# Attention's finished head pairs split one at a time, and one eviction of v moved behind a transpose

## The chip, the core and the metric

The kernel runs on one core of one Trainium2 chip. The metric is the device time of one execution in microseconds; the median of the runs shown is compared. The core has five engines that are used here: TensorE (PE in the profile; its weight loads are listed apart as PEld), VectorE (DVE), ScalarE (ACT), GpSimd (POOL) and SyncE (SP), which issues most DMAs. Each engine runs its own instructions in a fixed order and waits on semaphores for the others.

## The reference

A trunk of two layers over 512 tokens of width 1024: the first mixes with attention that has a forgetting gate, the second with a short gated convolution. A squared-ReLU MLP and a gated embedding follow in each. The change lies in the first layer's attention alone:

```python
def fox_attention(h, w_in, b_f, w_out):
    proj = h @ w_in                       # q, k, v and the forget logits
    ...
    log_f = jax.nn.log_sigmoid(f_logit)
    c = lax.cumsum(log_f, axis=1).transpose(0, 2, 1)
    ...
        s = jnp.einsum('bhqd,bhkd->bhqk', qb, k, preferred_element_type=jnp.float32)
        s = s + cb[..., :, None] - c[..., None, :]
        s = jnp.where(k_pos[None, :] <= q_pos[:, None], s, NEG_INF)
        pr = jax.nn.softmax(s, axis=-1)
        return jnp.einsum('bhqk,bhkd->bhqd', pr.astype(v.dtype), v)
    ...
    return o @ w_out
```

There are 16 heads of 64 columns, and the 512 queries are taken in four blocks of 128.

## The kernel before

All products are made exact by splitting: a 32-bit operand becomes a high half (hi), which ACT makes with a copy into the float32r type, and a low half (lo), the rest, which DVE makes with a subtraction. `mm3` (L266) then runs three matmuls, hi·hi, lo·hi and hi·lo. So each operand of a product costs one ACT and one DVE instruction, and each tile that leaves PSUM the same.

SBUF holds a pool of 70 pages of 128x512, from which nearly all tiles come; PSUM has 8 banks. Where an engine's order is not written out by hand (`tc.manual_schedule`), a scheduler orders the instructions when the kernel is built: earlier code has priority, an instruction whose inputs aren't expected yet lets later ones pass, and pages are handed out in the order of the code. `add_manual_dep(..., NoSync, ...)` (L634) fixes an order between two instructions of one engine without a semaphore.

*The start* (L700 to L732, order by hand on PE, DVE, ACT and POOL). The normalized input of four token blocks is turned by TensorE transposes (`turn_rows`, L696; `turned`, L334) and kept in two large tiles hT.hi and hT.lo (hTh and hTl in the profile; `keep`, L340). In between run the products for the first 272 columns of v (`values`, L461): block t of v is made in six groups of four matmuls (L479), and the transposes of block t + 1 stand before one of the groups (L476). Each block's result is evicted by `keep_v` (L485): a logit on DVE (L487), two casts on ACT (L500) and two subtractions on DVE (L502), none of which issues a DMA. `values` gives `keep_v` back, and the list `done_v` holds it until its turn. `prepare(n)` (L175) loads weights up to number n and splits them (L285 on ACT, L287 on DVE).

*The main loop* (L757 to L773). A step c takes one head and one of four key blocks (c // 4 and c % 4). `turn` (L576) transposes the softmax weights into a PSUM bank (pT, L579) and splits them into ph and pl (L583, that is L276 and L277). `mix` (L587), two steps later, multiplies them with v (L598, L599); after the fourth block the head's output leaves PSUM (L603, L604) and with every second head a pair is finished and enters the list `complete`. `scores` (L556) runs eight steps ahead (L563 to L572), `bias` (L538) further still. Between these, `next(main)` runs a piece of the generator `stream` (L656): first the q and k projections of the head pairs 1 to 7 (`project`, L510, eight products for k and eight for q, each followed by a `yield`; it evicts to kh, kl and qs), two pieces in each step, then the output product (`out_part`, L641) for token block 0, block 1, and at last pair 6.

The output product needs the finished pairs as a split operand. They are written over hT, whose row k holds the input of projection product k, so a pair's split must wait until the last projection has read that row. `split_o` (L614) does this only from the start of `out_part` (`streaming`): the casts of all finished pairs at once (L622), five of them at that point. `low_o` (L625) makes their subtractions (L629) when the first product needs one, and for the later pairs behind the `turn` of every fourth step (L767).

For the last eight steps (L758) TensorE's order is by hand too.

Of the kernel before, what the change touches and what calls it, by code (L numbers as in the profile page):

```python
# [8 lines left out]
F32 = mybir.dt.float32  # L9
F32R = mybir.dt.float32r  # L10
AF = mybir.ActivationFunctionType
ALU = mybir.AluOpType
# [3 lines left out]
P = 128  # L16
D = 1024
S = 512
# [3 lines left out]
KT = D // P  # L22
# [46 lines left out]
def trunk(ctx: ExitStack, tc, x, pT, g, gT, wv, wqk, bf, wo, wci, wcq, cw, wco, wup, wdn, wpp, wpg, out):  # L69
    nc = tc.nc  # L70
# [9 lines left out]
    def page(name, dtype=F32):  # L80
        return pages.tile([P, S], dtype, tag="pg", name=name)
# [78 lines left out]
    def derive(key):  # L160
        at, sums = recipes.pop(key)
        fetch(max(at.values()) + 1)
        B = {name: fetched[n][:, :S] for name, n in at.items()}
        for name, a, b, op in sums:
            t = page("_".join(str(u) for u in (*key, *name)))
            derived[(*key, *name)] = t
            B[name] = t[:, :S]
            ins = nc.gpsimd.tensor_tensor(out=B[name], in0=B[a], in1=B[b], op=op)  # L168
            if last_norm:
                tc.add_manual_dep(  # L170
                    ins.ins, last_norm.pop().ins.name,
                    mybir.DependencyInfo(mybir.DependencyClass.Sync, mybir.DependencyReason.DATA),
                )

    def prepare(upto, lows=None):  # L175
        while begun[0] < min(upto, len(order)):
            n = begun[0]
            begun[0] += 1
            key, at = order[n]
            for of in (key[:3], key[:2]):  # L180
                if of in recipes:
                    derive(of)
            hi, lo = page(f"wh{n}", F32R), page(f"wl{n}", F32R)
            if isinstance(at, tuple):
                raw, w = derived.pop(key), S
                eng = nc.gpsimd if (key[0] == "dn" and key[2] > 0) or key[-1] in ON_POOL else nc.vector
            else:
                fetch(at + 1)
                raw, eng, w = fetched[at], lows or nc.vector, loads[at].shape[-1]
                fetched[at] = None  # L190
            if key[0] in ("v", "qk"):
                split_gained(hi, lo, raw, w, key[2], eng, key[0] == "qk" or key[1] == 2)
            else:
                split(hi[:, :w], lo[:, :w], raw[:, :w], eng)
            ready[key] = Pair(hi[:, :w], lo[:, :w])
# [78 lines left out]
    def split(hi, lo, src, eng=nc.vector):  # L274

        nc.scalar.copy(hi, src)  # L276
        return eng.tensor_tensor(out=lo, in0=src, in1=hi.bitcast(F32), op=ALU.subtract)  # L277
# [135 lines left out]
    def attention(hT, first_x, b_f, work, by_hand):  # L413
# [94 lines left out]
        stacked, probs, outs, both = {}, {}, {}, {}  # L508

        def project(i):  # L510

            heads = [[page(f"{n}{i}_{e}", F32R) for n in ("qs", "kh", "kl")] for e in range(2)]
            stacked[i] = heads
            for s in (1, 0):
                ps = bank(f"qk{i}_{s}")
                for k in range(KT):
                    mm3(
                        ps, narrow("qk", i, k=k, c=s * P),
                        hT.at(lambda h: h[:, k, :]), k == 0, k == KT - 1,
                    )  # L520
                    if k < KT - 1:
                        yield
                for e in range(2):
                    a, b = slice(64 * e, 64 * e + 64), slice(64 - 64 * e, 128 - 64 * e)
                    q, kh, kl = heads[e]
                    if s == 0:
                        nc.scalar.mul(q[a, :S], ps[a, :], HD**-0.5)
                        nc.vector.scalar_tensor_tensor(
                            out=q[b, :S], in0=ps[a, :], scalar=HD**-0.5,
                            in1=q[a, :S].bitcast(F32), op0=ALU.mult, op1=ALU.subtract,  # L530
                        )
                    else:
                        split(kh[a, :S], kl[a, :S], ps[a, :])
                        for h in (kh, kl):
                            nc.sync.dma_start(h[b, :S].bitcast(F32), h[a, :S].bitcast(F32))
                yield
# [39 lines left out]
        def turn(h, j):  # L576
            ps = bank(f"pT{h}_{j}")
            for b in range(j, NB):
                nc.tensor.transpose(  # L579
                    ps[:, b * P : (b + 1) * P], probs[h][b][:, j * P : (j + 1) * P], ident  # L580
                )
            ph, pl = page(f"ph{h}_{j}", F32R), page(f"pl{h}_{j}", F32R)
            ins = split(ph[:, j * P : S], pl[:, j * P : S], ps[:, j * P :])  # L583
            weights[h, j] = (ph, pl)
            return ins

        def mix(h, j):  # L587

# [21 lines left out]

        banks_o = {}
        oT, complete, lows, streaming = [], [], [], [True]

        def split_o():  # L614

            if streaming:
                return
            if not oT:
                oT.append(turned_x)
            while complete:  # L620
                k = complete.pop(0)
                nc.scalar.copy(oT[0].hi[:, k, :], outs[k][:, :S])  # L622
                lows.append(k)

        def low_o(behind=None):  # L625

            while lows:
                k = lows.pop(0)
                ins = nc.vector.tensor_tensor(  # L629
                    out=oT[0].lo[:, k, :], in0=outs.pop(k)[:, :S],  # L630
                    in1=oT[0].hi[:, k, :].bitcast(F32), op=ALU.subtract,
                )
                if behind is not None:
                    tc.add_manual_dep(  # L634
                        ins.ins, behind.ins.name,
                        mybir.DependencyInfo(
                            mybir.DependencyClass.NoSync, mybir.DependencyReason.DATA
                        ),
                    )

        def out_part(ts, ks):  # L641

            streaming.clear()
            split_o()
            for k in ks:
                if k in lows:
                    low_o()
                for t in ts:
                    for n in range(2):
                        if (t, n) not in banks_o:  # L650
                            banks_o[t, n] = bank(f"o{n}_{t}")
                        w = wide("o", n, k, soon=O_SOON)
                        mm3(banks_o[t, n], tokens(oT[0], k, t), w, k == 0, False)
                        yield

        def stream():  # L656
            for i in range(1, KT):
                yield from project(i)
            yield from out_part((0,), range(6))
            yield from out_part((1,), range(6))  # L660
            prepare(where["o", 1, KT - 1] + 1)
            yield from out_part((0, 1), (6,))

        name = "n0"
        E, done_v = mybir.EngineType, []
# [30 lines left out]
        def turn_rows(t, hs):  # L696
            for n in range(2):
                keep(t, n, turned(t, n, hs[n], name), hT)

        with tc.manual_schedule(engines={E.PE, E.DVE, E.Activation, E.Pool}):  # L700
            work(12)
            r = inverse(0, mean_squares(0))
            prepare(2)
            hs = scale_rows(0, r)
            prepare(4)
            ps0 = [turned(0, n, hs[n], name) for n in range(2)]
            nc.scalar.copy(hT.hi[:, :4, :P], quads(ps0[0]))
            v = mean_squares(1)
            keep_low(0, ps0[0])
            prepare(5)  # L710
            r = inverse(1, v)
            nc.scalar.copy(hT.hi[:, 4:, :P], quads(ps0[1]))
            hs1 = scale_rows(1, r)
            prepare(KT)
            keep_low(1, ps0[1])
            v = mean_squares(2)
            r = inverse(2, v)
            done_v.append(values(0, 0, lambda: turn_rows(1, hs1)))
            hs2 = scale_rows(2, r)
            v = mean_squares(3)  # L720
            r = inverse(3, v)
            done_v.append(values(0, 1, lambda: turn_rows(2, hs2)))
            hs3 = scale_rows(3, r)
            prepare(KT + 2)
            done_v.pop(0)()
            done_v.append(values(0, 2, lambda: turn_rows(3, hs3)))
            prepare(KT + 4)
            done_v.pop(0)()
            prepare(KT + 6)
            done_v.append(values(0, 3, lambda: None))  # L730
            done_v.pop(0)()
            prepare(KT + 8)  # L732
# [5 lines left out]
            out=ones[:, :S], in_=ones[:, :S], compare_op=ALU.is_ge, fill=0.0, base=0,  # L738
# [403 lines left out]
    oT = lhs  # L1142
# [121 lines left out]
```

## Time and profile before

| | us |
|---|---|
| median of 3 runs | 1223.75 (1223.65 to 1224.49) |
| the profiled execution | 1223.06 |
| its span, first to last instruction | 1221.2 |
| mean granted TensorE clock | 0.998 |

In timelines a line has the start, the duration, the engine, the line of the kernel, the operation and its operands, output before input, then the number of instructions merged into the line and in brackets the idle time before it with what ended it. Matmuls have their columns in the shape (128x512). A row "x8" begins with the first of eight. A matmul's end is modelled, so the distance between starts tells more than the duration.

The start of v's products lies at 7 to 23 us, the main loop with the heads at about 80 to 225 us, the output product between 193 and 257 us.

### The profile page before, as it was taken

What the parts mean: (1) busy time and instruction counts of PE and PEld (TensorE: products, weight loads), DVE (VectorE), ACT (ScalarE), POOL (GpSimd) and SP (SyncE); (2) the same over time, 40 slices, a digit from 0 to 9 for tenths busy, and PEclk for the clock granted to TensorE, in tenths of its full rate; (3) what the DMA queues carried; (4) which work ended last, traced back from release to release, by engine and by line L of the source; (5) the groups of instructions that cost most, each with busy time, mean ns of one, the idle gap of its engine ahead of it and who ended that gap; (6) DMA issues with size and microseconds to landing.
All of it is one profiled execution on the core that took longest, in us unless ns stands there. A gap on an engine that the chain in (4) does not pass through costs nothing.

```text
span 1221.2 us, 18759 instructions
## 1 busy us (share of the span) xinstructions
PE 1209.6 (99%) x6202; PEld 1030.4 (84%) x6202; DVE 922.9 (76%) x1466; ACT 682.4 (56%) x1457; POOL 653.9 (54%) x612
## 2 busy tenths in 40 slices
PE   8999999999999999999999999999999999999997
PEld 7888887898888888888889999989888888888886
DVE  7668888586779766879877789766876787669873
ACT  5567778558634563455566434545756345635551
POOL 1036666154887777775213355216677878778210
PEclk9999999999999999999999999999999999999999
DMA  8556554623244224428123023552421443235401
GB/s 279 153 159 165 166 142 125 203 93 104 79 138 132 85 71 128 138 78 293 60 92 124 29 88 104 158 171 70 138 79 63 135 139 97 66 113 181 164 11 59
DMA packets 86161, 148.73 MB, mean 122 GB/s; under 512 B 10224, under 2 KB 17952, under 8 KB 86064
## 3 DMA queue, kind: packets, MB, share of 16 engines
q1 hardware_dynamic: 85488, 147.01, 39.2%
q8 instruction: 49, 0.80, 0.3%
q10 hardware_dynamic: 576, 0.53, 0.1%
q14 instruction: 48, 0.39, 0.1%
HBM read 136.93 MB, written 6.37 MB: 117 GB/s over the span
## 4 chain that ended last, share of the span: by engine, by line
PE 91%; issue 2%; DVE 2%; ACT 2%; POOL 1%; DMA 1%; POOLq 0%; DVEq 0%; ACTq 0%
PE up L269 9%; PE up L268 9%; PE up L270 9%; PE dn L268 8%; PE dn L269 8%; PE dn L270 8%; PE qk L269 2%; PE qk L270 2%; PE qk L268 2%; PE pg L268 2%; PE pg L269 2%; PE pg L270 2%; PE pT L579 1%; PE co L270 1%; PE co L269 1%
## 5 line engine op out<-in xcount | busy, mean ns | idle before, releaser
L277 DVE TENSOR_TENSOR wl<-raw,wh 128x512 fp32r<-128x512 f32 x346 | 347.4, 1049 | 14.2 <-ACT wh L276 13.5
L269 PE MATMUL up<-hTh,wl 128*128 128x512 f32 (+1 forms) x576 | 210.2, 365 | 0.0
L270 PE MATMUL up<-hTl,wh 128*128 128x512 f32 (+1 forms) x576 | 209.6, 365 | 0.0
L268 PE MATMUL up<-hTh,wh 128*128 128x512 f32 (+1 forms) x576 | 208.7, 366 | 0.0
L276 ACT CAST wh<-raw 128x512 fp32r<-128x512 f32 x346 | 189.4, 625 | 4.5 <-DVE xd L373 4.4
L924 ACT ACTIVATE r<-up 128x512 f32<-128x512 f32 (+1 forms) x72 | 39.4, 547 | 205.0 <-PE up L270 205.0
L277 POOL TENSOR_TENSOR wl<-dn_T,wh 128x512 fp32r<-128x512 f32 x96 | 132.5, 1412 | 30.0 <-ACT wh L276 30.0
L268 PEld LDWEIGHTS up<-hTh,wh 128*128 128x128 f32 x576 | 108.6, 189 | 17.7
L269 PEld LDWEIGHTS up<-hTh,wl 128*128 128x128 f32 x576 | 108.6, 189 | 17.5
L168 POOL TENSOR_TENSOR dn_T<-raw,raw 128x512 f32<-128x512 f32 x56 | 86.1, 1548 | 69.1 <-DMA raw<-in_wdn 56.7
L270 PEld LDWEIGHTS up<-hTl,wh 128*128 128x128 f32 x576 | 108.3, 189 | 17.4
L970 DVE TENSOR_TENSOR acc<-dn,acc 128x512 f32<-128x512 f32 x168 | 107.4, 679 | 16.0 <-PE dn L270 16.0
L168 POOL TENSOR_TENSOR dn_T<-raw,dn_T 128x512 f32<-128x512 f32 x56 | 91.9, 1640 | 2.2
L276 ACT CAST wh<-dn_T 128x512 fp32r<-128x512 f32 x112 | 61.4, 616 | 11.0 <-POOL dn_T L168 11.0
L277 DVE TENSOR_TENSOR A12l<-q,A12h 128x512 fp32r<-128x512 f32 x28 | 22.0, 787 | 54.4 <-ACT A12h L276 54.4
L984 POOL TENSOR_TENSOR acc<-acc,acc 128x512 f32<-128x512 f32 x28 | 46.9, 1706 | 9.9 <-DVE acc L970 9.9
L270 PE MATMUL qk<-hTl,wh 128*128 128x512 f32 x128 | 50.8, 397 | 0.0
L269 PE MATMUL qk<-hTh,wl 128*128 128x512 f32 x128 | 50.8, 397 | 0.0
L268 PE MATMUL qk<-hTh,wh 128*128 128x512 f32 x128 | 50.7, 396 | 0.0
L269 PE MATMUL pg<-wh,hTl 128*128 128x512 f32 x128 | 50.5, 394 | 0.0
L268 PE MATMUL pg<-wh,hTh 128*128 128x512 f32 x128 | 50.4, 394 | 0.0
L277 DVE TENSOR_TENSOR A11l<-q,A11h 128x256 fp32r<-128x256 f32 x28 | 22.9, 820 | 36.1 <-ACT A11h L276 36.1
(404 smaller groups left out, 3303.2 us busy)
## 6 DMA issues: line engine op xcount, KB each, us to landing
raw<-in_wup SPq DMA_DIRECT2D x128, 256.0 KB, 3.0
raw<-in_wdn SPq DMA_DIRECT2D x128, 256.0 KB, 2.9
raw<-in_wcq SPq DMA_DIRECT2D x36, 256.0 KB, 2.8
raw<-in_wqk SPq DMA_DIRECT2D x32, 256.0 KB, 4.0
raw<-in_wpg SPq DMA_DIRECT2D x32, 256.0 KB, 3.8
g<-in_g SPq DMA_DIRECT2D x22, 256.0 KB, 5.2
prl<-neg_c SPq DMA_DIRECT2D x16, 256.0 KB, 6.5
raw<-in_wo SPq DMA_DIRECT2D x16, 256.0 KB, 5.3
```

The lines of the kernel that those rows point to most:

```text
L168: ins = nc.gpsimd.tensor_tensor(out=B[name], in0=B[a], in1=B[b], op=op)
L268: nc.tensor.matmul(ps, a.hi, b.hi, start=start, stop=False)
L269: nc.tensor.matmul(ps, a.lo, b.hi, start=False, stop=False)
L270: nc.tensor.matmul(ps, a.hi, b.lo, start=False, stop=stop)
L276: nc.scalar.copy(hi, src)
L277: return eng.tensor_tensor(out=lo, in0=src, in1=hi.bitcast(F32), op=ALU.subtract)
L579: nc.tensor.transpose(ps[:, b * P : (b + 1) * P], probs[h][b][:, j * P : (j + 1) * P], ident)
L924: nc.scalar.activation(r[:, :n], ps[:, :n], AF.Relu)
L970: ins = nc.vector.tensor_tensor(out=a, in0=banks[s], in1=a, op=ALU.add)
L984: nc.gpsimd.tensor_tensor(out=a, in0=a, in1=acc[i, s][:, :S], op=ALU.add)
```

## The change

`turn` no longer calls the helper `split`; it issues the same two instructions itself and keeps the newest of each in `latest`. `split_o` takes a finished pair only up to number `reach[0]`; for the pairs 0 to 5 it queues the cast behind the newest ph cast on ACT and issues the subtraction at once, queued behind the newest pl subtraction on DVE. `reach` is set from within the last projection: after its q product of row 1 pair 0 may go, after row 3 pair 1, after row 5 pair 2, after row 7 pair 3; in `out_part` it is k + 3. Since two pieces run in each step, pairs 0 to 4 come up in steps 44 to 48, behind the turns of steps 43 to 47; pair 5 comes up in step 50. Pairs 6 and 7 are split as before. Separately, `keep_v` of block 0 is issued after block 2's products and the transposes of block 3 instead of before them.

```diff
@@ -580,9 +580,13 @@
             ph, pl = page(f"ph{h}_{j}", F32R), page(f"pl{h}_{j}", F32R)
-            ins = split(ph[:, j * P : S], pl[:, j * P : S], ps[:, j * P :])
+            latest[0] = nc.scalar.copy(ph[:, j * P : S], ps[:, j * P :])
+            latest[1] = nc.vector.tensor_tensor(
+                out=pl[:, j * P : S], in0=ps[:, j * P :], in1=ph[:, j * P : S].bitcast(F32),
+                op=ALU.subtract,
+            )
             weights[h, j] = (ph, pl)
-            return ins
+            return latest[1]
@@ -610,6 +614,7 @@
         oT, complete, lows, streaming = [], [], [], [True]
+        reach, latest = [0], [None, None]
@@ -617,12 +622,21 @@
-            while complete:
+            while complete and complete[0] <= reach[0]:
                 k = complete.pop(0)
-                nc.scalar.copy(oT[0].hi[:, k, :], outs[k][:, :S])
+                ins = nc.scalar.copy(oT[0].hi[:, k, :], outs[k][:, :S])
                 lows.append(k)
-
-        def low_o(behind=None):
+                if k < 6:
+                    behind(ins, latest[0])
+                    low_o(latest[1])
+
+        def behind(ins, other):
+            tc.add_manual_dep(
+                ins.ins, other.ins.name,
+                mybir.DependencyInfo(mybir.DependencyClass.NoSync, mybir.DependencyReason.DATA),
+            )
+
+        def low_o(after=None):
@@ -630,19 +644,16 @@
-                if behind is not None:
-                    tc.add_manual_dep(
-                        ins.ins, behind.ins.name,
-                        mybir.DependencyInfo(
-                            mybir.DependencyClass.NoSync, mybir.DependencyReason.DATA
-                        ),
-                    )
+                if after is not None:
+                    behind(ins, after)
 
         def out_part(ts, ks):
 
             streaming.clear()
             split_o()
             for k in ks:
+                reach[0] = k + 3
+                split_o()
                 if k in lows:
                     low_o()
@@ -655,7 +666,12 @@
         def stream():
             for i in range(1, KT):
-                yield from project(i)
+                for n, _ in enumerate(project(i)):
+                    yield
+                    if i == KT - 1 and n > KT:
+                        streaming.clear()
+                        reach[0] = (n - KT - 1) // 2
+                        split_o()
             yield from out_part((0,), range(6))
@@ -722,8 +738,8 @@
             prepare(KT + 2)
+            done_v.append(values(0, 2, lambda: turn_rows(3, hs3)))
             done_v.pop(0)()
-            done_v.append(values(0, 2, lambda: turn_rows(3, hs3)))
             prepare(KT + 4)
```

## The prediction

> **What bounds the kernel now.** I read the page first: engine busy times, then the chain of waits.
>
> ```profile
> PE 1209.6 (99%) x6202; PEld 1030.4 (84%) x6202; DVE 922.9 (76%) x1466; ACT 682.4 (56%) x1457; POOL 653.9 (54%) x612
> PE 91%; issue 2%; DVE 2%; ACT 2%; POOL 1%; DMA 1%; POOLq 0%; DVEq 0%; ACTq 0%
> ```
>
> TensorE is the bound, and the change leaves its instructions as they are. So only time in which TensorE stands still can be won. Busy time hides most of that, because a matmul's shown duration covers the gap behind it; I therefore read starts. Two neighbouring 512-column products start 0.23 us apart (193.48 and 193.71 below), so 256 columns are worth 0.11 and 128 columns 0.06. Then I went to the timelines at the two places that the diff touches.
>
> At the end of attention (PE, then ACT, then DVE):
>
> ```profile
> 182.03 0.27 PE L579 MATMUL pT<-ident,prl 128*128 128x128 f32 x1
> ...
> 189.88 0.27 PE L564 MATMUL sc<-kl,qs 128*128 128x128 f32 x1
> 190.22 0.39 PE L598 MATMUL ps_o<-ph,v 128*128 128x256 f32 x1
> 190.82 0.33 PE L579 MATMUL pT<-ident,pr 128*128 128x128 f32 x1 [0.21 <-DVE nmx L566]
> ...
> 191.55 0.39 PE L563 MATMUL sc<-kh,qs 128*128 128x256 f32 x1 [0.18 <-DVE kl L277]
> 191.77 0.28 PE L564 MATMUL sc<-kl,qs 128*128 128x256 f32 x1
> 192.00 0.39 PE L599 MATMUL ps_o<-pl,v 128*128 128x256 f32 x1
> ...
> 193.48 0.39 PE L268 MATMUL o<-wh,hTh 128*128 128x512 f32 x1
> 193.71 0.40 PE L269 MATMUL o<-wh,hTl 128*128 128x512 f32 x1
> ...
> 199.23 0.40 PE L270 MATMUL o<-wl,hTh 128*128 128x512 f32 x1
> ```
>
> ```profile
> 183.63 0.62 ACT L622 CAST hTh<-oT 128x512 fp32r<-128x512 f32 x1 [0.56 <-PE qk L269]
> ...
> 185.91 1.13 ACT L622 CAST hTh<-oT 128x512 fp32r<-128x512 f32 x2
> ...
> 187.42 1.14 ACT L622 CAST hTh<-oT 128x512 fp32r<-128x512 f32 x2
> ...
> 189.80 1.03 ACT L276 CAST ph<-pT 128x256 fp32r<-128x256 f32 x3
> ...
> 197.15 0.37 ACT L276 CAST ph<-pT 128x256 fp32r<-128x256 f32 x1
> ```
>
> ```profile
> 184.28 0.69 DVE L629 TENSOR_TENSOR hTl<-oT,hTh 128x512 fp32r<-128x512 f32 x1 [0.45 <-PE qk L269]
> ...
> 187.01 1.29 DVE L629 TENSOR_TENSOR hTl<-oT,hTh 128x512 fp32r<-128x512 f32 x2
> 188.22 0.68 DVE L277 TENSOR_TENSOR kl<-qk,kh 64x512 fp32r<-64x512 f32 x1
> 188.82 1.28 DVE L629 TENSOR_TENSOR hTl<-oT,hTh 128x512 fp32r<-128x512 f32 x2
> ...
> 190.80 0.69 DVE L277 TENSOR_TENSOR kl<-qk,kh 64x512 fp32r<-64x512 f32 x1
> ...
> 193.57 0.16 DVE L571 RECIPROCAL rs<-sm 128x1 f32<-128x1 f32 x1 [0.56 <-ACT prr L570]
> ...
> 197.16 0.69 DVE L528 SCALAR_TENSOR_TENSOR qs<-qk,qs 64x512 fp32r<-64x512 f32 x1 [0.45 <-ACT qs L527]
> ...
> 199.54 0.29 DVE L277 TENSOR_TENSOR pl<-pT,ph 128x128 fp32r<-128x128 f32 x1 [1.24 <-ACT ph L276]
> ```
>
> What to see: the five splits (five casts on L622, five subtractions on L629) stand between 183.6 and 190.1. The transposes of one turn ended at 182.3 (182.03 + 0.27), yet their cast ph runs only at 189.80, behind all five casts, and then three turns come at once. On DVE four of the five subtractions stand ahead of the two kl subtractions of the last projection. From 189.88 to 192.00 TensorE does 0.06 + 0.11 + 3 × 0.11 + 2 × 0.11 = 0.7 us of work in 2.1 us: 1.4 us are lost.
>
> **Part one: v's eviction behind the last transposes.**
>
> ```profile
> 16.08 1.03 PE L337 MATMUL n_p<-ident,n_h 128*128 128x128 f32 x8
> ...
> 19.48 0.67 PE L479 MATMUL v<-wl,hTh 128*128 128x272 f32 x4
> 19.99 1.03 PE L337 MATMUL n_p<-ident,n_h 128*128 128x128 f32 x8
> 20.78 0.74 PE L479 MATMUL v<-wh,hTl 128*128 128x272 f32 x4
> 21.83 0.77 PE L479 MATMUL v<-wh,hTh 128*128 128x272 f32 x4 [0.30 <-ACT hTh L276]
> ```
>
> ```profile
> 16.72 1.08 ACT L276 CAST hTh<-n_p 128x512 fp32r<-128x512 f32 x2 [3.32 <-PE n_p L337]
> ...
> 20.85 0.43 ACT L500 CAST v<-v 128x128 fp32r<-128x128 f32 x2 [1.83 <-DVE logit L487]
> 21.17 1.10 ACT L276 CAST hTh<-n_p 128x512 fp32r<-128x512 f32 x2
> ```
>
> ```profile
> 19.33 1.41 DVE L287 SCALAR_TENSOR_TENSOR wl<-raw,first_g,wh 128x512 fp32r<-128x512 f32 x2
> ...
> 21.81 1.29 DVE L277 TENSOR_TENSOR hTl<-n_p,hTh 128x512 fp32r<-128x512 f32 x2
> ```
>
> Four 272-column products take 0.51 us (19.48 to 19.99), so TensorE is free at 20.78 + 0.51 = 21.29 and stands until 21.83: 0.54 us. It waits for hTh, whose cast stands on ACT behind v's two casts, which stand behind the logit on DVE. The block before shows the free case: transposes at 16.08, cast at 16.72, 0.64 us later. So the cast can start at 19.99 + 0.64 = 20.63 instead of 21.17, and hTh is there at about 21.29, when TensorE is free. Removed: 0.54 us.
>
> The price: the moved step (one logit, two casts, two subtractions, no DMA) now stands behind hTl, 1.29 us on DVE, and the next weight casts on ACT stand behind it, as do the loads that wait for their raw buffers: some 0.8 us later. What covers them is six groups of 0.51 us of the last v block and the two weights whose low halves end at 20.74 (19.33 + 1.41), each good for 3 × 0.23 = 0.7 us per block of tokens. That is 4.5 us from 21.29 with one block alone. Cover gone, the lateness of 0.8 would eat the gain: bounds −0.54 and +0.3. I take **−0.5**, since the cover is five times the delay.
>
> **Part two: the splits one by one.** Nothing is added or removed: five casts at 0.57 us (1.13 / 2) and five subtractions at 0.65 us (1.29 / 2). They move behind the turns of steps 43 to 47, released as the last projection passes their rows of hT.
>
> The stall at 190: the kl subtractions then have no split ahead of them (four × 0.65 = 2.6 us of DVE and four × 0.57 = 2.3 us of ACT gone from 185.9 to 190.1), so ph comes earlier by up to 2.6 us. I value the stall of 1.4 at −1.2, leaving 0.2 for the handovers that every turn has; bounds −1.4 and 0 (if the projection's products, which filled TensorE meanwhile, are merely spread otherwise).
>
> Later there is more:
>
> ```profile
> 205.89 0.28 PE L564 MATMUL sc<-kl,qs 128*128 128x256 f32 x1
> 206.46 0.33 PE L579 MATMUL pT<-ident,prr 128*128 128x128 f32 x1 [0.29 <-DVE pl L277]
> ...
> 210.92 0.40 PE L269 MATMUL o<-wh,hTl 128*128 128x512 f32 x1
> 211.67 0.51 PE L270 MATMUL o<-wl,hTh 128*128 128x512 f32 x1 [0.35 <-DVE wl L277]
> ```
>
> Here TensorE loses 0.46 (0.57 − 0.11) and 0.52 (0.75 − 0.23) because DVE is late, while DVE had stood idle for 1.24 us at 199.54. The reason is the run of output products from 193.48 to 199.23, four pairs' worth. After the change a fourth pair may enter only behind the turn whose ph runs at 197.15. Its six products, 6 × 0.23 = 1.4 us, then stand behind that turn instead of ahead; attention and with it DVE restart up to 1.4 us sooner, and these products are left over for the thin steps after 199.5. Bounds: −1.4 and, if DVE must first do the postponed subtractions, +3.2 (five × 0.65). DVE's idle rows above (0.56 + 0.45 + 1.24 = 2.2 us) take in most of those, so I value it near the lower end, **−1.1**.
>
> The new waits: each cast is queued behind the newest ph on ACT, each subtraction behind the newest pl on DVE. Behind them stand the exponentials of later scores and the next ph. The sixth pair's subtraction moves ahead by some turns, inside a stretch where DVE is full anyway: nothing, or ±0.65, one subtraction.
>
> A rule that speaks against this part: the row at 183.63 shows ACT standing 0.56 us before the first split, for a projection product that still reads that row of hT. The Trainium skill, "TensorE: Matmul & The Clock Gate", section "Architectural detail: the array is 16× 32×32, not 1× 128×128", says that ACT and DVE serve their queues strictly in order, TensorE alone pulling weight loads ahead. By that rule a split that waits so holds ph and the exponentials too; its result is the third rival. This row agrees: ACT did nothing meanwhile.
>
> **Sum.** The profiled execution took 1223.06 us, 1.86 around its span of 1221.2; the median is 0.69 above it. 1223.06 − 0.5 − 1.2 − 1.1 = 1220.3, and 1220.3 + 0.69 = **1221.0 us** against 1223.75. Nothing downstream absorbs it: TensorE is the chain from there on.
>
> **Rivals.**
> 1. *The splits aren't the cause at 199 and later.* DVE is simply full there, and the lows move from one full stretch into the next. For it: 2.2 us of idle against 3.2 us of lows. Then only 0.5 + 1.2 come: 1222.0.
> 2. *The change doesn't do what it says.* The splits stand between other work already (one, two, two), and TensorE's order stays the same: only v's part counts, 1223.2. Against it: ph at 189.80 follows the last of them.
> 3. *The splits wait at the head of ACT.* Each of the five waits 0.56 us as the first did: +2.8, with v's −0.5 and no other gain 1226.05. Against it: four of the five showed no such wait.
> 4. *The output products lose their pairs (slower).* Place: the run from 193.48. With three pairs released instead of four it is 1.4 us too short for the wait that it covers, and five lows of 0.65 stand ahead of pl instead of in gaps: 1.4 + 3.25 = 4.65; less 0.5 and 1.2 it is +2.95, 1226.7. It decides as soon as DVE's 2.2 us of idle are not where the lows arrive. For it: the lows are tied to pl, the very chain that starts the next turn. Against: shorter delay at 190 leaves projection products over, each 0.7 us, for the same gap.
> 5. *All stalls go* (the lows fit in gaps, the later stalls vanish whole, 1.4 more than the sum): 1219.6.
>
> **How the numbers follow.** About 0.2%, 2.45 us, is what a measurement of this kernel can tell from no change: below 1221.3 is faster, above 1226.2 slower. My forecast gets 0.50 (its own range 1220.0 to 1222.0; 0.35 of it below 1221.3), rival five 0.05, rival one 0.11, rival two 0.06, rival three 0.06 (half of it above 1226.2), rival four 0.22. Faster: 0.35 + 0.05 = 0.40. Slower: 0.22 + 0.03 = 0.25. The same: 0.35. The range 1219.5 to 1226.3 leaves out a little of rival five and most of rival four, some 0.2; it is wide because of the bounds +3.2 and −1.4 on the postponed lows.
>
> **What would show it.** Right: the first v product of the last block starts near 21.3 and ACT's hTh cast ahead of v's casts; the first split behind a ph, none between the kh casts; no gap over 0.3 us between 187 and 192 by the old clock; the run of output products cut to three pairs and no DVE idle over 1 us around 199. Wrong: a gap of over 1 us in front of an output product that waits for hTl, an idle ACT in front of L622 several times, or DVE busy without a break from 190 to 215 while TensorE loses as much as before. If the time is above 1223.2, part two's sign was wrong.

## The result and the profile after

| | before | after |
|---|---|---|
| median, us (12 runs each) | 1223.81 (1223.65 to 1224.63) | 1221.28 (1220.75 to 1222.23) |
| profiled execution, us | 1223.06 | 1220.75 |
| its span, us | 1221.2 | 1219.0 |

The ratio is 0.9979, with a 95% interval from 0.9971 to 0.9988: 2.53 us less by the medians, 2.31 by the profiled executions. The page's busy times and chain hardly differ, which is how a change reads that only takes gaps out of the bounding engine:

```profile
PE 1208.5 (99%) x6202; PEld 1030.3 (85%) x6202; DVE 919.2 (75%) x1466; ACT 684.0 (56%) x1457; POOL 653.8 (54%) x612
PE 92%; issue 2%; DVE 2%; ACT 2%; POOL 1%; DMA 0%; POOLq 0%; DVEq 0%; ACTq 0%
```

TensorE runs the same products, so the start of the same product in two traces tells how far one kernel is ahead of the other. This table is used for all that follows: start in before minus start in the kernel named, in us.

| product | before, start | after | v alone | splits alone | unqueued | casts free | at once | two by two |
|---|---|---|---|---|---|---|---|---|
| first projection product | 59.55 | 0.64 | -0.18 | 0.02 | 0.19 | 0.45 | 0.37 | -0.14 |
| transposes of the last turn | 221.17 | 2.15 | -0.59 | 1.54 | -0.33 | 0.15 | -4.16 | -0.69 |
| between the two | | +1.51 | -0.41 | +1.52 | -0.52 | -0.30 | -4.53 | -0.55 |

Two executions of one text (the O_SOON 3 of below) gave +0.76 and +0.59 between the two products, so a difference of 0.2 is not read as an effect here, and a run that comes out at -0.3 or -0.5 is read as one that won none of the 1.5. Whole times of single executions are given, but say less: those of the kernel before alone went from 1223.1 to 1226.0.

In the changed kernel the first output product is 1.69 ahead (193.48 against 191.79) and the end 2.2 (the spans). So the gain has three places: 0.6 by the first projection product, 1.05 from there to the first output product (0.64 to 1.69), 0.46 from there to the last turn (1.69 to 2.15). The code lines have moved by a few: the casts and subtractions of the splits, L622 and L629 before, are L627 and L643 now, and ph and pl have lines of their own, L583 and L584.

The timeline at the last block's transposes, TensorE and then ACT (start, duration, engine, line, operation, and in brackets the idle time before and what ended it):

```profile
20.73 0.74 PE L479 MATMUL v<-wh,hTl 128*128 128x272 f32 x4
21.32 0.68 PE L479 MATMUL v<-wh,hTh 128*128 128x272 f32 x4
```

```profile
20.58 1.08 ACT L276 CAST hTh<-n_p 128x512 fp32r<-128x512 f32 x2 [1.58 <-PE n_p L337]
22.60 0.44 ACT L500 CAST v<-v 128x128 fp32r<-128x128 f32 x2 [0.95 <-DVE logit L487]
```

The second group of v products follows the first after 0.59 us, where there had been 1.05, and hTh now stands ahead of v's casts.

The timeline at 190, ACT, DVE and TensorE:

```profile
184.10 0.56 ACT L276 CAST kh<-qk 64x512 fp32r<-64x512 f32 x1
...
186.12 0.58 ACT L276 CAST kh<-qk 64x512 fp32r<-64x512 f32 x1
186.73 0.38 ACT L583 CAST ph<-pT 128x256 fp32r<-128x256 f32 x1
187.84 0.27 ACT L583 CAST ph<-pT 128x128 fp32r<-128x128 f32 x1 [0.74 <-PE pT L579]
188.00 0.62 ACT L627 CAST hTh<-oT 128x512 fp32r<-128x512 f32 x1
```

```profile
185.26 0.68 DVE L277 TENSOR_TENSOR kl<-qk,kh 64x512 fp32r<-64x512 f32 x1
...
186.73 0.69 DVE L277 TENSOR_TENSOR kl<-qk,kh 64x512 fp32r<-64x512 f32 x1 [0.45 <-ACT kh L276]
...
188.66 0.69 DVE L643 TENSOR_TENSOR hTl<-oT,hTh 128x512 fp32r<-128x512 f32 x1 [0.23 <-ACT hTh L627]
```

```profile
191.31 0.34 PE L564 MATMUL sc<-kl,qs 128*128 128x384 f32 x1
191.79 0.50 PE L268 MATMUL o<-wh,hTh 128*128 128x512 f32 x1
...
196.17 0.39 PE L270 MATMUL o<-wl,hTh 128*128 128x512 f32 x1
```

The first split stands behind a ph, both kl are done by 187.4 instead of 191.5, and the stall of 1.4 us is gone. The ph that ran at 189.80 runs at 186.73; without the 0.64 of the start that is 2.4 us sooner. A new gap of 0.31 us stands in front of the first output product (191.79 - 191.31 less 0.17 for 384 columns). The run of output products has 18 of them, three pairs' worth, up to 196.17; before there were 24.

Two stretches by engine, before and then after: the run of output products, and the last turns behind it. Columns: the stretch, its length, busy time and instructions of PE, PEld, DVE, ACT, POOL, then the granted TensorE clock, the DMA share and GB/s.

```profile
194.00:200.00 6.00, 6.00 (x29) 4.89 (x28) 4.02 (x12) 3.55 (x9) 3.64 (x6) 1.00 0.68 150
203.00:216.00 13.00, 12.24 (x65) 8.80 (x64) 12.47 (x39) 12.27 (x32) 9.21 (x12) 1.00 0.32 84
```

```profile
192.00:198.00 6.00, 6.00 (x32) 4.99 (x32) 5.77 (x17) 5.37 (x15) 4.26 (x8) 1.00 0.69 137
201.00:214.00 13.00, 12.41 (x68) 9.16 (x67) 12.81 (x39) 12.25 (x33) 9.80 (x11) 1.00 0.29 87
```

DVE was busy 4.02 of 6 us beside the run and is now busy 5.77; behind it, it was busy 12.47 of 13 and is now busy 12.81. The idle time was filled, and the stretch behind stayed as full as it was. There TensorE still loses:

```profile
203.44 0.30 PE L603 MATMUL ps_o<-pl,v 128*128 128x128 f32 x1
203.87 0.38 PE L563 MATMUL sc<-kh,qs 128*128 128x256 f32 x1
...
205.07 0.49 PE L270 MATMUL o<-wl,hTh 128*128 128x512 f32 x1
205.74 0.50 PE L602 MATMUL ps_o<-ph,v 128*128 128x512 f32 x1 [0.17 <-DVE nmx L566]
...
208.86 0.40 PE L269 MATMUL o<-wh,hTl 128*128 128x512 f32 x1
209.53 0.50 PE L270 MATMUL o<-wl,hTh 128*128 128x512 f32 x1 [0.28 <-DVE wl L277]
```

By the starts that is 0.37 + 0.44 + 0.44 = 1.25 us in the gaps of over 0.2; the kernel before had 1.51 of them in the same part.

### The profile page after: what moved, and what is told of

It is laid out like the page before. It is cut to its first block, busy times and chain, and to the rows that moved or that the text cites. A ratio compares the mean times of both kernels' runs of the same rounds, so it can differ in the third digit from the quotient of the medians.

```text
span 1219.0 us, 18773 instructions
## 1 busy us (share of the span) xinstructions
PE 1208.5 (99%) x6202; PEld 1030.3 (85%) x6202; DVE 919.2 (75%) x1466; ACT 684.0 (56%) x1457; POOL 653.8 (54%) x612
## 4 chain that ended last, share of the span: by engine, by line
PE 92%; issue 2%; DVE 2%; ACT 2%; POOL 1%; DMA 0%; POOLq 0%; DVEq 0%; ACTq 0%
PE up L268 9%; PE up L270 9%; PE up L269 9%; PE dn L268 8%; PE dn L270 8%; PE dn L269 8%; PE qk L270 2%; PE qk L269 2%; PE qk L268 2%; PE pg L268 2%; PE pg L270 2%; PE pg L269 2%; PE pT L579 1%; PE co L269 1%; PE co L268 1%
## 5 line engine op out<-in xcount | busy, mean ns | idle before, releaser
L270 PE MATMUL pg<-wl,hTh 128*128 128x512 f32 x128 | 50.2, 392 | 0.0
```

The source lines that it names most:

```text
L270: nc.tensor.matmul(ps, a.hi, b.lo, start=False, stop=stop)
```

## The experiments

The theory: the gain at 190 and after comes from the order on ACT and DVE (splits ahead of kh, kl and ph), and it needs the splits both spread and queued. Rivals: it is v's part that shifts everything; or the postponed lows, or the late output weights, set the rest. Each diff is against the changed kernel, unless it says otherwise.

**v alone** and **splits alone** (the two parts apart; the first is the kernel before with this edit, the second the changed kernel without it):

```diff
+            done_v.append(values(0, 2, lambda: turn_rows(3, hs3)))
             done_v.pop(0)()
-            done_v.append(values(0, 2, lambda: turn_rows(3, hs3)))
```

> The kernel before with v's eviction moved and the splits left as they were. Sum of stalls: TensorE is ahead by 0.6 us from 21.3 us on, still by 0.6 at the last transposes of attention, and the stall at 190 is as before (1.4 us lost); span 1220.6, some 0.6 under the kernel before. Rival, the stretch in which DVE is full takes it back: 0.6 ahead at the first projection, nothing left after 215, span 1221.2.

> The changed kernel with v's eviction where it was. Sum of stalls: no difference up to 180, 1.4 us won between 188 and 192, 1.5 to 1.6 at the last transposes, span 1219.6 to 1219.7. Rival, the two parts help each other (DVE is ahead by v's 0.6 when the splits come): less than 1.2 won, span over 1220. Other rival, v's part is not needed: span 1219.0.

v alone: 1223.05 us (10 runs) against 1223.44 (19), ratio 0.9995 with an interval from 0.9985 to 1.0004. Its trace began 0.76 us late, since x came late in that run, and was only 0.18 behind at the first projection product: the edit won 0.58, as in the changed kernel. Then 0.45 was lost again by the first output product, at 190, on DVE:

```profile
187.33 1.38 DVE L629 TENSOR_TENSOR hTl<-oT,hTh 128x512 fp32r<-128x512 f32 x2
188.63 0.67 DVE L277 TENSOR_TENSOR kl<-qk,kh 64x512 fp32r<-64x512 f32 x1
189.24 1.49 DVE L629 TENSOR_TENSOR hTl<-oT,hTh 128x512 fp32r<-128x512 f32 x2
...
191.43 0.69 DVE L277 TENSOR_TENSOR kl<-qk,kh 64x512 fp32r<-64x512 f32 x1
```

The second kl comes 0.63 later than before's, of which 0.18 is the late start; the same pairs of subtractions took 1.29 and 1.28 there. A further 0.44 went around 256 us, in front of the first up products. So the 0.58 is won where it arises, and in this execution as much and more was lost again behind it. But the profiled execution was the slowest of the ten, 0.90 above their median, and by the medians 0.39 is left, within the noise: how much of the term stays without the other part is open.

Splits alone: 1222.01 us (10 runs) against 1223.44, ratio 0.9986 (0.9977 to 0.9996). It won 1.08 up to the first output product and 0.44 from there to the last turn, against 1.05 and 0.46 in the changed kernel; 0.47 was given back later, 0.2 before the first down products and 0.3 in the second layer. The second and third terms therefore belong to the splits, and are no effect of v's part.

**unqueued** (the splits are released at the same steps, but nothing ties them to the newest ph and pl):

```diff
-                    behind(ins, latest[0])
-                    low_o(latest[1])
+                    low_o()
```

> The changed kernel without the queueing of the splits behind the newest turn: they are released one at a time by reach, but may run earlier where the scheduler sees a gap. If it is their place on DVE ahead of the kl subtractions that cost 1.4 us, some of them go back there: 0.5 to 1.4 us lost at 190 again, span 1219.5 to 1220.4. If releasing them one at a time is enough, the trace is as in the changed kernel and the span 1219.0.

One execution, 1223.18 us, span 1221.4, and 0.52 lost between the first projection product and the last turn. ACT's order is that of the kernel before, one, two and two casts ahead of the ph:

```profile
183.44 0.62 ACT L627 CAST hTh<-oT 128x512 fp32r<-128x512 f32 x1 [0.42 <-PE qk L269]
...
185.72 1.13 ACT L627 CAST hTh<-oT 128x512 fp32r<-128x512 f32 x2
186.75 0.58 ACT L276 CAST kh<-qk 64x512 fp32r<-64x512 f32 x1
187.23 1.14 ACT L627 CAST hTh<-oT 128x512 fp32r<-128x512 f32 x2
...
189.69 1.03 ACT L583 CAST ph<-pT 128x256 fp32r<-128x256 f32 x3
```

Releasing the splits one by one wins nothing by itself: without the queueing they go back to their old places.

**casts free** (only the subtractions are queued):

```diff
-                    behind(ins, latest[0])
                     low_o(latest[1])
```

> The changed kernel with only the subtractions queued behind the newest pl; the casts on ACT may run as early as the scheduler likes. Counted from the first projection product to the last transposes of attention, the changed kernel won 1.5 us. If the subtractions on DVE ahead of kl were what cost 1.4 us, the casts alone ahead of kh cost little: 1.2 to 1.5 us won. If ACT's part counts as much, half of it or less: under 0.8 us won.

1224.14 us in one execution, beside 1224.38 for the kernel before on that chip; 0.30 lost. The subtractions stand behind pl as in the changed kernel, but the casts are back at 185.45 and 186.95, two each, with kh at 186.48 and 188.73; the second kl comes at 189.96 instead of 186.73. The casts on ACT ahead of kh are enough to cost the gain, though DVE has no split in its way:

```profile
186.95 1.14 ACT L627 CAST hTh<-oT 128x512 fp32r<-128x512 f32 x2
...
188.73 0.58 ACT L276 CAST kh<-qk 64x512 fp32r<-64x512 f32 x1
```

**at once** (all five released together at the start of the output products, queued behind the newest turn):

```diff
-        reach, latest = [0], [None, None]
+        reach, latest = [9], [None, None]
...
-                reach[0] = k + 3
-                split_o()
...
-                for n, _ in enumerate(project(i)):
...
+                yield from project(i)
```

> The changed kernel without the early release: all five pairs are split where the output product starts, queued behind the newest turn. If only their place ahead of kl cost time, the stall at 190 stays away and the span is 1219.0 to 1219.3. If the output product needs them early, five subtractions of 0.65 us come in a row behind pl in front of the run of output products: TensorE loses 1 to 3 us between 192 and 200, span 1220 to 1222.

1228.51 us in one execution, span 1226.8: 4.5 lost. kl is early here too (185.93 and 187.40). But no output product is ready when the new head's first turns need cover, on ACT, DVE and TensorE:

```profile
195.62 0.37 ACT L583 CAST ph<-pT 128x256 fp32r<-128x256 f32 x1
195.88 2.70 ACT L627 CAST hTh<-oT 128x512 fp32r<-128x512 f32 x5
```

```profile
196.69 3.48 DVE L643 TENSOR_TENSOR hTl<-oT,hTh 128x512 fp32r<-128x512 f32 x5
```

```profile
196.04 0.38 PE L602 MATMUL ps_o<-ph,v 128*128 128x256 f32 x1 [2.48 <-ACT ph L583]
```

TensorE stands 2.48 us, and then the five subtractions hold the turns' pl for 3.48. Something else adds to it: behind this wait TensorE's granted clock is 0.5 for 3.41 us, from 197.04 to 200.46, which at half speed makes up to 1.7 us of the loss (a stretch of it, columns as above):

```profile
197.10:200.40 3.30, 3.30 (x15) 2.89 (x13) 3.30 (x7) 2.23 (x5) 3.30 (x4) 0.50 0.42 98
```

This is the fourth rival's mechanism. Its price can't be held against the 4.5 as it stands: the stall at 190 is gone here too, so the rival would lose 4.65 less 1.2, or 3.45, between the two products, and it had no term for the clock. The spread is needed as well as the queue.

**two by two** (two pairs released in each step of the last projection):

```diff
-                        reach[0] = (n - KT - 1) // 2
+                        reach[0] = n - KT
```

> The changed kernel with two pairs released in each step instead of one, still queued: all five pairs come behind the turns of steps 43 to 46, so four pairs, 24 output products, may run ahead of head 11's late turn as before. If the shorter run of three pairs was worth something (my term of 1.1, of which the trace shows little), 0.3 us or more less is won than the 1.5 of the changed kernel, and DVE idles over 1 us near 197. If the run's length is worth nothing, 1.4 to 1.6 us won. If two subtractions in a row delay pl, TensorE loses up to 1.3 us between 189 and 192.

1223.62 us in one execution beside 1224.38; 0.55 lost. The splits come as three and two, and TensorE waits twice behind them (on DVE the pl and the nmx that it waits for each stand behind a pair of subtractions):

```profile
192.60 0.50 PE L603 MATMUL ps_o<-pl,v 128*128 128x512 f32 x1 [0.81 <-DVE pl L584]
...
194.16 0.50 PE L268 MATMUL o<-wh,hTh 128*128 128x512 f32 x1 [0.54 <-DVE nmx L566]
```

The run of output products has 24 again (194.16 to 199.84), and DVE is idle 0.78 and 0.94 us around 200, as before; the second of these:

```profile
200.10 0.29 DVE L584 TENSOR_TENSOR pl<-pT,ph 128x128 fp32r<-128x128 f32 x1 [0.94 <-ACT ph L583]
```

That ties the length of the run to DVE's idle time, the step on which the third term rested. The two waits cost the 0.55 already up to the first output product (0.54); from there to the last turn nothing was won, where the run of 18 won 0.46.

**Output weights** (is the rest lost to a late wl?). On GpSimd, for pairs 4 and 5; and made ready earlier, O_SOON 3 and 2 instead of 1:

```diff
+                if key[0] == "o" and key[2] in (4, 5):
+                    eng = nc.gpsimd
```

```diff
-O_SOON = 1
+O_SOON = 3
```

> The changed kernel with the low halves of the output weights for pairs 4 and 5 (four subtractions of 0.65 us, 2.6 us) made by GpSimd instead of DVE. If DVE's full stretch from 201 to 214 is what keeps the later stalls (about 2 us above the normal small gaps), these fall by 1 us or more: 2.5 us won instead of 1.5. If the chain of turn, cast and subtraction has the same length whatever DVE's load, nothing changes; if GpSimd's subtraction (1.4 us, and behind the normalizations of the softmax) comes too late, output products wait for it and up to 1 us is lost.

> The changed kernel with the output weights prepared three ahead instead of one. The wait of an output product for its weight's low half (0.44 us at 209) goes: 0.3 to 0.5 us more won. If DVE's fullness decides, the earlier subtractions displace pl and as much is lost at the turns: the same 1.5 us won, within 0.2.

> The same text as the experiment that makes the output product's weights ready two steps sooner (O_SOON = 3), now timed in rounds beside the kernel before. In its single look attention ended 0.75 us later than in the changed kernel and the whole program 0.1 us earlier by the span, since about 1 us came back between 277 and 295 us, at the start of the feed-forward part. If that return belongs to the kernel (other instruction order there), the median stands 0.8 us or more under the changed kernel's distance to before: some 3.3 us under before, ratio 0.9973. If it was a chance of that one run (loads arriving earlier), the median is 1.7 to 2.0 us under before, ratio 0.9985, a worse kernel than the changed one (0.9979).

> The changed kernel with the output product's weights ready one step sooner (O_SOON = 2 in place of 1; it was 1 before and after). In the changed kernel TensorE still stood 0.44 us at 209.5 for one weight's low half (wl on DVE). If the remaining stalls of attention come from such weights being late, the one step wins that 0.4 us: 2.9 us under before. If they come from DVE being full from 201 to 214, the weight's subtraction only pushes another of DVE's steps back and the stalls move: 2.0 to 2.5 us under before, and the trace shows new gaps for nmx or pl where the one for wl went.

On GpSimd: 1224.65 us in one execution beside 1224.38, and 2.0 lost between the two landmarks. One such subtraction takes 1.26 us there against 0.69 on DVE, and it stands between the row scalings of the turns, so it is late:

```profile
210.95 0.49 PE L272 MATMUL o<-wl,hTh 128*128 128x512 f32 x1 [0.82 <-POOL wl L279]
212.76 0.50 PE L272 MATMUL o<-wl,hTh 128*128 128x512 f32 x1 [1.32 <-POOL wl L279]
```

O_SOON 3: 1220.84 in one execution, then a median of 1220.87 (10 runs, against 1223.72), ratio 0.9976 (0.9967 to 0.9985). O_SOON 2: 1221.75, ratio 0.9984 (0.9975 to 0.9994). Inside attention both are worse than the changed kernel: +0.76 and +0.59 in the two traces of 3, +0.30 in that of 2, against +1.51. The gap for wl at 209.5 is gone, but gaps of 0.70 and 1.10 stand behind it, in front of steps of the turns, at 212.8 (3) and 215.8 (2): the waits are only passed on. What brings the time back is elsewhere: all three win 1.05 on the kernel before between 280 and 590 us, in the first down products, where the changed kernel wins 0.07. There the products' inputs come too late for TensorE in the changed kernel, such as A12h, whose cast ends at 285.18 (ACT, then TensorE):

```profile
284.56 0.62 ACT L276 CAST A12h<-q 128x512 fp32r<-128x512 f32 x1
```

```profile
284.69 0.40 PE L270 MATMUL dn<-wl,S1h 128*128 128x512 f32 x1
285.24 1.20 PE L268 MATMUL dn<-wh,A12h 128*128 128x512 f32 x4
```

**Loads on GpSimd's queue** (does the late load of g, for which DVE waits 0.90 us at 235.56, cause that 1.05?). First all twelve loads of xb and g, then only g and xb of blocks 0 and 1:

```diff
-            nc.sync.dma_start(
+            (nc.gpsimd if l == 0 and i in (1, 2) else nc.sync).dma_start(
...
-            eng = nc.scalar if name == "xa" and n else nc.sync
+            eng = nc.scalar if name == "xa" and n else nc.gpsimd if name == "xb" else nc.sync
```

> The changed kernel with the twelve loads of the first output block (eight xb, four g) issued from GpSimd's queue, which has nothing to do there, and no longer from SyncE's, where they stand behind five weight loads (209.51, 15.76 us for the five). In the changed kernel DVE waits 0.90 us for g in front of its first om product at 235.56, and some 45 us later TensorE loses 1.0 us in the first down products, between 283 and 288, whose inputs hang on that chain. In the two kernels with earlier output weights (O_SOON 3 and 2) these loads went out earlier, attention ended later, and that 1.0 us was not lost. If the late g load is the cause, the row of om starts near 234.7 without a wait for DMA, the losses at 283 to 288 shrink by 0.7 to 1.0 us with attention as before: some 3.3 us under before, ratio 0.9972. If the loss has another cause (the sums on GpSimd, ACT's order), attention and the losses stay and the time stays 2.5 us under before, ratio 0.9979. If issuing from GpSimd itself costs (twelve issues in front of the next rows on that engine), the first or_r_v on GpSimd starts later than 229.9 and the time is above 1221.3.

> As the run with all twelve loads on GpSimd's queue, but only the four g and the xb of the first two token blocks go there; xb of blocks 2 and 3 stay on SyncE. In the run with all twelve, the wait for g went, om started 2.4 us earlier and the 1.0 us at 283 to 288 was no longer lost, but in the order of instructions the om and xb steps of blocks 2 and 3 had been moved behind the casts and subtractions of the first blocks' transposes, and TensorE then stood 4.1 us at 262.4. With only half of them moved, TensorE's order is that of the changed kernel, and the steps of blocks 2 and 3 stand where they stood there. If the order alone cost the time, there is no stall over 0.5 us at 262, om starts at 234.7 or before, and 0.7 to 1.0 us of the losses at 283 to 288 are won: 3.3 us under before, ratio 0.9973. If issuing loads from GpSimd is what costs, the stall at 262 stays and the time is above 1223.

All twelve: 1226.96 us (9 runs) against 1223.51, ratio 1.0027 (1.0017 to 1.0037). om starts 2.4 us earlier, at 233.12, but DVE's new order puts the residual step of block 2 behind the first blocks' subtractions, and TensorE stands 4.1 us behind the transposes that start at 262.4. The granted clock is 0.5 for 3.41 us after that stall too, so not all of this run's loss is the order's. Between 280 and 590 us it wins 0.75 on the kernel before, but behind such a stall that says little. Half of them: 1221.13 (11 runs) against 1223.34, ratio 0.9981 (0.9972 to 0.9990). There is no wait for g and no stall at 262; the loss in the first down products stays, and behind attention only 0.1 is won. So the late g is not the cause. What the traces show instead is the order around 250, on DVE and ACT, after and then O_SOON 3 as timed:

```profile
249.85 0.74 DVE L373 SCALAR_TENSOR_TENSOR xb<-om,or_r_y,xb 128x512 f32<-128x512 f32 x1
250.51 0.68 DVE L277 TENSOR_TENSOR hTl<-n_p,hTh 128x512 fp32r<-128x512 f32 x1
251.11 0.73 DVE L373 SCALAR_TENSOR_TENSOR xb<-om,or_r_y,xb 128x512 f32<-128x512 f32 x1
```

```profile
249.63 1.41 DVE L373 SCALAR_TENSOR_TENSOR xb<-om,or_r_y,xb 128x512 f32<-128x512 f32 x2
...
251.76 1.29 DVE L277 TENSOR_TENSOR hTl<-n_p,hTh 128x512 fp32r<-128x512 f32 x2 [0.73 <-ACT hTh L276]
```

With O_SOON 3 and 2 the two residual steps come together, ahead of hTl; in the changed kernel and with half of the loads moved, a subtraction stands between them. The normalised rows then come at the same time (254.96 and 255.05), although attention ended 1.2 us later with O_SOON 3. This fits the 1.05, but no run changed that order alone; it stays open. Nor is any version shown to beat the changed kernel: 0.9976 and 0.9979 lie inside each other's intervals.

## Why the prediction was right in its time, and which term was not

| term | forecast | measured |
|---|---|---|
| v's eviction | -0.5 | -0.59 (0.05 at the last transposes to 0.64); alone -0.58 |
| stall at 190 | -1.2 | -1.05 (0.64 to 1.69); alone -1.08 |
| later stalls | -1.1 | -0.46 (1.69 to 2.15); alone -0.44 |

*v's eviction* went as worked out, stall and cover alike. What the sum left out is whether the gain lasts: in the trace of v alone it was lost again at 190 and later, while that run's medians keep 0.39. Whether the term hangs on the second one is not shown.

*The stall at 190* vanished as forecast, for the reason given: with the splits out of the order kh, kl and ph come early, and unqueued and casts free, which put the casts back, lose it again. 1.4 us were won and 0.31 came back as one new gap in front of the first output product, so the 0.2 kept for handovers was nearly right. One reading of the text is off without touching the sum: three of the five subtractions stand ahead of the first kl and all five ahead of the second, not four ahead of both; four is the number that stands between 187 and 190.1.

*The later stalls* are the mis-sized term. The mechanism was right: the run has three pairs, DVE's idle 1.24 us is gone, its busy share beside the run went from 67 to 96% (4.02 and 5.77 of 6), and two by two shows the idle time come back with the fourth pair. Its size was not. The text took the earlier restart, 1.4 us, as time won, on the ground that the postponed subtractions would fit into idle time. They did, and behind them DVE was as full as before (12.47 and 12.81 of 13): the restart moved work forward, but the gaps of the stretch from 201 to 214 stayed for the most part. Of the two stalls that the text had named, the one for wl kept 0.44 of 0.52, and in place of the one of 0.46 stands one of 0.44 in front of another step (205.07 to 205.74). That DVE's own work sets this stretch is argued from its busy time and from the gaps that move when a weight's subtraction does; no run emptied DVE there without delaying something else. The value stood too near the lower end of its bounds, -1.4 and +3.2. The sign that the text had named for this, DVE busy without a break while TensorE loses as much, was seen in good part: 1.25 of 1.51 us.

*The sum.* The terms forecast 2.8 us, the trace shows 2.1; the medians, at 2.53, lie nearer the forecast, since the profiled execution of before stands 0.75 under its median and that of after 0.53. So 0.2 of the agreement is the choice of executions, and the third term's miss of 0.64 is larger than what the medians show of it: that part is luck. The range says little as well, since 1219.5 to 1226.3 holds the times of rivals one, two, three and five. What carries the prediction are the first two terms, which came true in size and in their rows. At 1221.28 the time lies on the text's own border between faster and the same, 1221.3.

*The rivals.* Rival one, 1222.0, described the third term best and was 0.7 too high for the median. Rival two (the splits do nothing) is ruled out by splits alone. Rival three's wait did not arise: none of the five casts has an idle ACT in front of it. Its rule holds all the same: in every run that puts casts ahead of kh or ph, these wait their turn. Here the Trainium skill, "TensorE: Matmul & The Clock Gate", section "Architectural detail: the array is 16× 32×32, not 1× 128×128", by which ACT and DVE serve their queues strictly in order, agrees with the traces as far as they tell: in unqueued and casts free kh and ph run behind the casts that stand ahead of them (in casts free the casts at 186.95 for 1.14 us, an exponential behind them, kh at 188.73). Rival four's mechanism was seen only in the run with all five at once, where all five lows come in one piece and no output product is ready to cover them; the change avoids it by spreading.

## What to carry to other kernels

Work that is free to run early may stand ahead of a chain in an engine's order, and it then delays the chain although nothing depends on it. Two things are needed to take it out: a tie to the chain's newest step, and a release in single pieces; either alone won nothing here, and the tie without the single release lost 4.5 us. Before a moved idle time is counted as won, read whether the engine is full in the stretch behind it: filling the gap only pays until that stretch begins.

## What the runs showed of the hardware that was not expected

TensorE's clock fell after a long wait. In two traces TensorE stood for over 2 us inside the program, 2.48 us (at once) and 3.93 us (all twelve loads moved). In both, and in none of the other twelve traces, whose longest wait is 1.32 us (output weights on GpSimd), the granted clock was then 0.5 for 3.41 us. So a wait of that length cost up to 1.7 us more than itself. Where between 1.32 and 2.48 us this begins, these runs do not show.

GpSimd took longer beside two of DVE's subtractions back to back. The scaling of a 128x256 row (pr) on GpSimd, before, with v alone, and after:

```profile
188.44 2.45 POOL L572 TENSOR_SCALAR pr<-pr,rs 128x256 f32<-128x256 f32 x1
```

```profile
188.15 1.88 POOL L572 TENSOR_SCALAR pr<-pr,rs 128x256 f32<-128x256 f32 x1
```

```profile
188.03 0.92 POOL L572 TENSOR_SCALAR pr<-pr,rs 128x256 f32<-128x256 f32 x1
```

In the first two it overlaps the pairs of hTl at 188.82 and 189.24; in the third one single hTl at 188.66 falls beside its last 0.3 us. The subtraction's part is read from the overlap alone; no run separated it. The Trainium skill, "SBUF — State Buffer", section "Who interferes with whom", says that a DVE instruction with two inputs in SBUF contends with a GpSimd instruction that reads SBUF; the rows of before agree. The row of after shows no loss, but the next scaling there (128x384, from 188.94), which the rest of that hTl overlaps, took 1.53 us against 1.24 for the same shape in before (190.87).

The start differs from execution to execution. The load of x for block 1 (xc) ends an idle time of DVE of up to 0.8 us in some profiles, and of none in before and after; with half of the loads moved it is 0.77 us, in front of the step at 9.12. The whole rest is later by as much (TensorE's transposes of that block at 11.55 instead of 10.74). That is why advances are counted here from the first projection product, and why spans of single executions are not compared to less than 0.8 us.
